# Thirty-six more small matmuls on a constant, around the first key tile of the first mixer

## Chip, core and metric

One core of a Trainium2 chip runs the whole program. The metric is the device time of one execution in microseconds, as the median of several runs. The engines are TensorE (PE; its weight loads are shown apart as PEld), VectorE (DVE), ScalarE (ACT), GpSimd (POOL) and SyncE (SP), which starts the transfers.

## What is computed

A decoder trunk of two layers for one sequence of 512 tokens and width 1024. The change lies in the first layer's mixer, sparse attention with an indexer: every query scores all earlier keys with eight small index heads, keeps the best 128 of them and attends to those.

```python
proj = rms_norm(x, norm_mix) @ w_in
q, k, v, qi, ki, wi, qm = _split(proj, A_SIZES)
logits = jnp.einsum('bqhd,bsd->bqhs', qib, ki)
score = jnp.einsum('bqhs,bqh->bqs', jax.nn.relu(logits), wib)
score = jnp.where(key_pos <= t_pos, score, NEG)
_, idx = lax.top_k(score, n_sel)
# attention of q over the chosen k, v; four more heads attend to 256 memory tokens
x = x + jnp.concatenate([mix, mo], axis=-1) @ w_out
x = x + swiglu_ffn(rms_norm(x, norm_ffn), w_gate_up, w_down)
```

All inputs and the output are float32.

## The kernel before

Activations lie transposed, 128 features by 512 tokens a tile, eight tiles (`KT`) for the width. A projection to 128 output features is eight accumulation steps over `KT` into one PSUM bank. There are two ways to do it. `fp32_steps` (L207) multiplies in float32 directly; the trace has two records for each such matmul. `proj_steps` (L235 to L237) splits weight and activation into a high and a low part, `wh`, `wl`, `xh`, `xl`, rounded for the fast float32 mode, and does three matmuls for each of the eight steps: `xh·wh`, `xl·wh`, `xh·wl`. The split of a weight is `_split2`: ScalarE casts the high part (L48), VectorE or GpSimd subtracts to get the low part (L51). `proj_steps` is a generator that stops after every second step, so after six matmuls, a quarter of the product.

`layer0` runs so: 14 small matmuls of `ones` by `ones` (L738) while the first loads are under way; five index projections in float32 (`product`, results `pk`, `pq`, `p1`, `p2`, `p3`); meanwhile the scaled input `x` is split into `xh` and `xl` (`halves`). Then comes the first tile of attention keys: `rope_steps(K, kb[:, 0], tag="O")` makes the product of 24 matmuls into the PSUM bank `psO` and turns it by the rotary angles (L374 to L384: five ScalarE copies out of PSUM, then GpSimd). The first four stops of `steps` are that product; it is the loop over `itertools.islice(steps, 4)`.

After it, the value product (`token_major`, L441 to L443, into `psT`) is woven with the index logits (`logits`, L452 into `psacc` and `psS`): for each of four pairs of heads and three query blocks two matmul groups, a ScalarE relu in PSUM (L789) and a VectorE update of the score (L791, L793). Between them stand the sums of squares of the memory tokens (L278, L256 to L265) and the row made of them (L288, L290). When the score is complete, VectorE runs 16 rounds of top-k (L727, L728) while PE does the next projections, the memory heads and the queries.

The order on PE is the order of the code. The other engines' order comes from a scheduler that lays the program out by a model of its times; added PE work can shift what it puts where. PSUM tags are pools: `acc` has two banks, `S` three, `T` two, `O` one. Split weights rotate through three `wh` and three `wl` buffers, raw weights through two `wf` buffers.

Of the kernel before, what the change touches and what calls it, by code (L numbers as in the profile page):

```python
# [53 lines left out]
def _weave(a, b, na=1, nb=1):  # L54

    live = True
    while live:
        live = False
        for g, n in ((a, na), (b, nb)):
            for _ in range(n):  # L60
                if next(g, g) is not g:
                    live = True


class _Trunk:
# [667 lines left out]

    def layer0(self):
        nc, mm = self.nc, self.nc.tensor.matmul
        idle = self.psum("T")
        for _ in range(14):
            mm(idle[:, :128], self.ones, self.ones, start=True, stop=True)  # L738
        x, parts = self.scaled(0)
        ws = itertools.chain(self.first, self.plain_chunks("in0", [2, 3, 4]))  # L740

# [35 lines left out]
        def logits(j):  # L777
            for i in (1, 2, 3):
                n = (i + 1) * 128
                sc = score[i]  # L780
                q = slice(j * 512 + i * 128, j * 512 + (i + 1) * 128)
                tag = ("S", "acc")[(j + i) % 2]
                ps = [self.psum(tag) for _ in range(2)]
                self.scores([(ps[s][:, :n], qi, None, ki, None, slice(s * 64, s * 64 + 64), q, slice(0, n))
                             for s in range(2)])
                for s in range(2):
                    t = ps[s]
                    w = wi[:, i, 2 * j + s:2 * j + s + 1]
                    nc.scalar.activation(t[:, :n], t[:, :n], AF.Relu)  # L789
                    if j + s == 0:  # L790
                        nc.vector.tensor_scalar(sc[:, :n], t[:, :n], w, None, op0=ALU.mult)  # L791
                    else:
                        nc.vector.scalar_tensor_tensor(sc[:, :n], t[:, :n], w, sc[:, :n], op0=ALU.mult, op1=ALU.add)  # L793
                if j == 3:
                    nc.gpsimd.affine_select(out=sc[:, i * 128:n], in_=sc[:, i * 128:n], pattern=[[-1, 128]],
                                            compare_op=ALU.is_ge, fill=NEG, base=0, channel_multiplier=1)
                yield 1
# [26 lines left out]
        steps = itertools.chain(rope_steps(K, kb[:, 0], tag="O"), value_steps())  # L824
        mem_parts = self.memory_squares(mem)
        every = itertools.chain.from_iterable(logits(j) for j in range(4))
        for _ in itertools.islice(steps, 4):
            pass
        _weave(itertools.islice(steps, 3), itertools.islice(every, 6), nb=2)
        self.mem_cols = self.ssq_cols(mem_parts, n=2, keep=True)  # L830
        _weave(itertools.islice(steps, 3), every, nb=2)
# [552 lines left out]
```

## Time and profile before

| | us |
|---|---|
| median of 3 runs | 1238.37 (1238.08 to 1239.43) |
| profiled execution | 1237.89 |
| its span, first to last instruction | 1236.0 |
| PE busy | 1196.5 (97%) |
| PEld busy | 944.8 (76%) |
| DVE busy | 529.3 (43%) |
| ACT busy | 484.1 (39%) |
| POOL busy | 350.2 (28%) |

The mean granted TensorE clock is 0.992 of full speed. PE's busy share is close to the span, so the places to read are the few in which PE waits, and the stretches in which its clock is granted at half. A matmul's recorded time is longer than the step to the next one, because matmuls overlap in the pipeline; the step from start to start is what it costs in a row of matmuls.

### The profile page before, as it was taken

The page shows a single profiled execution, that of the slowest core. Times are in us where ns is not written, and L with a number is a line of the kernel's source. Part 1 is how long each engine was busy: PE and PEld are TensorE (multiplying, and loading weights), DVE is VectorE, ACT ScalarE, POOL GpSimd, SP SyncE. Part 2 cuts the span into 40 slices and gives each one's busy share as a digit, 9 for nine tenths or more (in the row PEclk, how much of TensorE's full clock was granted, in tenths as well). Part 3 has the DMA queues.
Part 4 walks back from the last instruction along what each step waited for, and adds up shares of the span by engine and source line. Part 5 has one row for each costly group of instructions (what it writes and reads, how often), then busy time and mean ns, then how long its engine had stood idle before and what let it go on. Part 6 is the DMA issues. An engine that isn't in the chain of part 4 may idle for free.

```text
span 1236.0 us, 14342 instructions
## 1 busy us (share of the span) xinstructions
PE 1196.5 (97%) x5624; PEld 944.8 (76%) x5624; DVE 529.3 (43%) x1022; ACT 484.1 (39%) x852; POOL 350.2 (28%) x220
## 2 busy tenths in 40 slices
PE   9799899999999999999999999998999999999997
PEld 5367576578788888888888778886788888888886
DVE  4769724547433333332224543559433333331112
ACT  3663584424423323222222776545323223222222
POOL 0444453245222122212222323324322122211222
PEclk9899999999999999999999999999999999999999
DMA  5313103102322222222233121211222222222221
GB/s 189 130 38 132 57 35 95 59 34 92 110 76 99 102 102 103 79 96 94 94 115 113 58 69 34 83 55 69 91 82 100 103 103 101 77 87 94 94 94 69
DMA packets 29185, 108.36 MB, mean 88 GB/s; under 512 B 2494, under 2 KB 11582, under 8 KB 20670
## 3 DMA queue, kind: packets, MB, share of 16 engines
q1 hardware_dynamic: 28574, 106.93, 24.6%
q8 instruction: 44, 0.72, 0.2%
q10 hardware_dynamic: 544, 0.52, 0.1%
q14 instruction: 23, 0.19, 0.0%
HBM read 104.43 MB, written 3.01 MB: 87 GB/s over the span
## 4 chain that ended last, share of the span: by engine, by line
PE 77%; DVE 10%; DMA 4%; issue 4%; ACT 3%; POOL 2%; SPq 0%; DVEq 0%; POOLq 0%; ACTq 0%
PE psS L249 5%; PE psS L247 5%; PE psS L248 5%; PE psT L249 3%; PE psT L247 3%; PE psT L248 3%; PE psacc L249 3%; PE psacc L247 3%; PE psacc L248 3%; PE psacc L222 3%; PE psacc L224 3%; PE psacc L223 3%; PE psS L222 3%; PE psS L224 3%; PE psS L223 3%
## 5 line engine op out<-in xcount | busy, mean ns | idle before, releaser
L51 POOL TENSOR_TENSOR wl<-wf,wh 128x1024 fp32r<-128x1024 f32 x92 | 222.7, 2422 | 618.9 <-ACT wh L48 567.4
L48 ACT CAST wh<-wf 128x1024 fp32r<-128x1024 f32 (+1 forms) x163 | 167.4, 1030 | 505.4 <-issue 156.1
L51 DVE TENSOR_TENSOR wl<-wf,wh 128x1024 fp32r<-128x1024 f32 (+1 forms) x84 | 99.4, 1184 | 80.0 <-ACT wh L48 80.0
L249 PE MATMUL psS<-xh,wl 128*128 128x512 f32 x272 | 106.9, 393 | 0.0
L247 PE MATMUL psS<-xh,wh 128*128 128x512 f32 x272 | 106.5, 392 | 0.0
L248 PE MATMUL psS<-xl,wh 128*128 128x512 f32 x272 | 106.1, 390 | 0.0
L247 PE MATMUL psacc<-xh,wh 128*128 128x512 f32 x192 | 75.5, 393 | 0.6 <-DVE xT L653 0.6
L247 PE MATMUL psT<-xh,wh 128*128 128x512 f32 x192 | 75.5, 393 | 0.0
L249 PE MATMUL psT<-xh,wl 128*128 128x512 f32 x192 | 75.5, 393 | 0.0
L249 PE MATMUL psacc<-xh,wl 128*128 128x512 f32 x192 | 75.5, 393 | 0.0
L248 PE MATMUL psT<-xl,wh 128*128 128x512 f32 x192 | 74.9, 390 | 0.0
L248 PE MATMUL psacc<-xl,wh 128*128 128x512 f32 x192 | 74.9, 390 | 0.0
L316 POOL TENSOR_TENSOR ssq<-ssq,t 128x512 f32<-128x512 f32 (+1 forms) x31 | 41.0, 1322 | 96.6 <-ACT t L306 61.1
L248 PEld LDWEIGHTS psS<-xl,wh 128*128 128x128 f32 x272 | 51.1, 188 | 11.6
L249 PEld LDWEIGHTS psS<-xh,wl 128*128 128x128 f32 x272 | 51.1, 188 | 11.1
L247 PEld LDWEIGHTS psS<-xh,wh 128*128 128x128 f32 x272 | 51.1, 188 | 10.7
L235 PE MATMUL psacc<-xh,wh 128*128 128x512 f32 x136 | 58.1, 428 | 0.0
L668 DVE TENSOR_TENSOR raw<-psacc,R 128x512 f32<-128x512 f32 x22 | 15.2, 691 | 96.9 <-PE psacc L249 96.9
L237 PE MATMUL psacc<-xh,wl 128*128 128x512 f32 x136 | 54.1, 398 | 0.0
L236 PE MATMUL psacc<-xl,wh 128*128 128x512 f32 x136 | 54.0, 397 | 0.0
L653 DVE TENSOR_TENSOR xT<-xT,psacc 128x512 f32<-128x512 f32 x44 | 30.0, 683 | 39.0 <-PE psacc L224 38.9
L247 PEld LDWEIGHTS psacc<-xh,wh 128*128 128x128 f32 x192 | 36.1, 188 | 8.7 <-issue 1.2
(320 smaller groups left out, 2628.8 us busy)
## 6 DMA issues: line engine op xcount, KB each, us to landing
wf<-in_gu SPq DMA_DIRECT2D x44, 1024.0 KB
wf<-in_dn SPq DMA_DIRECT2D x16, 1024.0 KB
wf<-in_in SPq DMA_DIRECT2D x12, 1024.0 KB
wf<-in_dn SPq DMA_DIRECT2D x16, 384.0 KB
wf<-in_v SPq DMA_DIRECT2D x3, 1024.0 KB
wf<-in_in SPq DMA_DIRECT2D x5, 512.0 KB
xT<-in_x SPq DMA_DIRECT2D x8, 256.0 KB
wf<-in_mk SPq DMA_DIRECT2D x2, 1024.0 KB
```

The source lines that it names most:

```text
L48: nc.scalar.copy(hi, src)
L51: lo_engine.tensor_tensor(out=lo, in0=src, in1=hi.bitcast(F32), op=ALU.subtract)
L222: mm(out, wh[k], xh[k], start=first and k == 0, stop=False)
L223: mm(out, wh[k], xl[k], start=False, stop=False)
L224: mm(out, wl[k], xh[k], start=False, stop=last and k == n - 1)
L235: mm(out, wh[:, s], xh[k], start=k == 0, stop=False)
L236: mm(out, wh[:, s], xl[k], start=False, stop=False)
L237: mm(out, wl[:, s], xh[k], start=False, stop=k == KT - 1)
L247: mm(out, wh[:, s], xh[k], start=k == 0, stop=False)
L248: mm(out, wh[:, s], xl[k], start=False, stop=False)
L249: mm(out, wl[:, s], xh[k], start=False, stop=k == KT - 1)
L316: engine.tensor_tensor(out=parts[part], in0=parts[part], in1=sq, op=ALU.add)
```

## The change

The small matmuls of `ones` by `ones` become a helper, `keep_awake(tag, n)`, which takes a PSUM bank of the given tag and does `n` of them. It is called as before at the start (14 in `psT`), then with 16 in a bank of `acc` ahead of the first key tile's product, and with 5 after each quarter of that product.

```diff
     def layer0(self):
         nc, mm = self.nc, self.nc.tensor.matmul
-        idle = self.psum("T")
-        for _ in range(14):
-            mm(idle[:, :128], self.ones, self.ones, start=True, stop=True)
+        def keep_awake(tag, n):
+
+            idle = self.psum(tag)
+            for _ in range(n):
+                mm(idle[:, :128], self.ones, self.ones, start=True, stop=True)
+
+        keep_awake("T", 14)
...
         every = itertools.chain.from_iterable(logits(j) for j in range(4))
+        keep_awake("acc", 16)
         for _ in itertools.islice(steps, 4):
-            pass
+            keep_awake("acc", 5)
         _weave(itertools.islice(steps, 3), itertools.islice(every, 6), nb=2)
```

Lines behind the change are four or five further down in the changed kernel. On PE, at the end of the index projections (`psT<-xg,wf` is the last of them, `psO` the key product), the program now reads:

```order
L207 MATMUL psT<-xg,wf 128x512 x8
L740 MATMUL psacc<-ones 128x128 x16
L235 MATMUL psO<-xh,wh 128x512
L236 MATMUL psO<-xl,wh 128x512
L237 MATMUL psO<-xh,wl 128x512
L235 MATMUL psO<-xh,wh 128x512
L236 MATMUL psO<-xl,wh 128x512
L237 MATMUL psO<-xh,wl 128x512
L740 MATMUL psacc<-ones 128x128 x5
```

The six rows of the product and the five behind them come four times in all, and the fourth five stand ahead of the first `L441`. The first of the sixteen, and the first of the second, third and fourth five, waits for PE's own earlier work on its bank. Before, the `L740` rows are not there and the rest is the same.

On ScalarE, behind the casts of the value weights, before (names in brackets are the engines and transfers that an instruction waits for):

```order
L48 CAST wh<-wf 128x1024 [waits DMAHW6_49]
L48 CAST wh<-wf 128x1024
L374 COPY raw<-psO 128x512 [waits DMAHW4_49,PE_49,Pool_49]
L379 COPY raw<-psO 32x512 [waits DMAHW5_49,Pool_49]
L379 COPY raw<-psO 32x512 x3
L48 CAST wh<-wf 128x1024 [waits DMAHW7_49,DVE_49]
L789 ACTIVATE psacc<-psacc 128x256 [waits PE_49] x2
```

and in the change, where the copies and the relus have other line numbers in part:

```order
L48 CAST wh<-wf 128x1024 [waits DMAHW6_49]
L48 CAST wh<-wf 128x1024
L48 CAST wh<-wf 128x1024 [waits DMAHW7_49,DVE_49,PE_49]
L374 COPY raw<-psO 128x512 [waits DMAHW4_49,PE_49,Pool_49]
L379 COPY raw<-psO 32x512 [waits DMAHW5_49,Pool_49]
L379 COPY raw<-psO 32x512 x3
L793 ACTIVATE psacc<-psacc 128x256 [waits PE_49] x2
```

The cast for the second key tile has moved ahead of the five copies out of `psO`, and now waits for PE as well.

On VectorE, in the logits of the third pair of heads (`rs_q` and `rs_keep` belong to the memory tokens' norm), before:

```order
L263 TENSOR_TENSOR rs_q<-rs_keep 128x2
L793 SCALAR_TENSOR_TENSOR score<-psacc,wi,score 128x256
L264 SCALAR_TENSOR_TENSOR rs_q<-rs_v,rs_q 128x2
L793 SCALAR_TENSOR_TENSOR score<-psacc,wi,score 128x256
L265 SCALAR_TENSOR_TENSOR rs_keep<-rs_q,rs_keep 128x2
L793 SCALAR_TENSOR_TENSOR score<-psS,wi,score 128x384
L263 TENSOR_TENSOR rs_q<-rs_keep 128x2
L793 SCALAR_TENSOR_TENSOR score<-psS,wi,score 128x384
L264 SCALAR_TENSOR_TENSOR rs_q<-rs_v,rs_q 128x2
L265 SCALAR_TENSOR_TENSOR rs_keep<-rs_q,rs_keep 128x2
L288 TENSOR_SCALAR raw<-ident,rs_keep 128x128 x2
```

and in the change:

```order
L263 TENSOR_TENSOR rs_q<-rs_keep 128x2
L264 SCALAR_TENSOR_TENSOR rs_q<-rs_v,rs_q 128x2
L265 SCALAR_TENSOR_TENSOR rs_keep<-rs_q,rs_keep 128x2
L263 TENSOR_TENSOR rs_q<-rs_keep 128x2
L264 SCALAR_TENSOR_TENSOR rs_q<-rs_v,rs_q 128x2
L265 SCALAR_TENSOR_TENSOR rs_keep<-rs_q,rs_keep 128x2
L288 TENSOR_SCALAR raw<-ident,rs_keep 128x128 x2
L797 SCALAR_TENSOR_TENSOR score<-psacc,wi,score 128x256 x2
L797 SCALAR_TENSOR_TENSOR score<-psS,wi,score 128x384 x2
```

The four score updates have moved behind the whole column chain. GpSimd does the low part of the second key tile's weight ahead of the turn of the first key tile; ScalarE also does one copy of values earlier among scalings of the memory tokens. All other rows of all engines, and SyncE's transfers, keep their order.

## Rows read from the trace of the kernel before

**Rows 1.** The page, part 1: busy us, share of the span, instructions.

```profile
PE 1196.5 (97%) x5624; PEld 944.8 (76%) x5624; DVE 529.3 (43%) x1022; ACT 484.1 (39%) x852; POOL 350.2 (28%) x220
```

**Rows 2.** Waits of PE: us in total, times, longest.

```profile
PE psT L469 <- ACT frow L485: 4.3, 3, 2.8
PE psO L235 <- ACT wh L48: 4.2, 1, 4.2
PE psO L237 <- DVE wl L51: 2.8, 1, 2.8
```

**Rows 3.** Timeline of PE: start us, us, operation, [idle before <- what ended it].

```profile
36.97 0.41 PE L770 MATMUL psS<-ident,o 8*128 8x8 f32 x4
38.91 8.83 PE L207 MATMUL psT<-xg,wf 128*128 128x512 f32 x16 [1.53 <-DMA wf<-in_in]
51.91 0.50 PE L235 MATMUL psO<-xh,wh 128*128 128x512 f32 x1 [4.17 <-ACT wh L48]
...
55.45 0.80 PE L237 MATMUL psO<-xh,wl 128*128 128x512 f32 x1 [2.80 <-DVE wl L51]
...
59.73 0.39 PE L235 MATMUL psO<-xh,wh 128*128 128x512 f32 x1
...
62.48 0.28 PE L441 MATMUL psT<-wh,xh 128*128 128x256 f32 x1
```

**Rows 4.** Windows: busy us (count) by engine, PEclk, DMA share, GB/s.

```profile
38.90:42.40 3.50, 3.49 (x5) 1.43 (x6) 2.39 (x3) 3.39 (x7) 0.72 (x1) 0.53 0.30 114
...
55.45:59.45 4.00, 4.00 (x9) 3.13 (x10) 4.00 (x6) 0.00 (x0) 3.02 (x3) 0.50 0.74 264
59.53:62.48 2.95, 2.95 (x14) 2.42 (x13) 1.23 (x2) 2.00 (x2) 0.21 (x1) 1.00 0.85 347
...
146.40:149.10 2.70, 0.00 (x0) 0.00 (x0) 0.00 (x0) 2.64 (x6) 2.70 (x2) 1.00 0.00 0
149.10:152.00 2.90, 2.85 (x14) 1.78 (x16) 1.38 (x2) 1.12 (x2) 2.88 (x4) 1.00 0.98 315
```

**Rows 5.** Small and fp32 matmuls: PE timeline (two rows), windows of `ones` on PE.

```profile
1.12 5.20 PE L738 MATMUL psT<-ones 128*128 128x128 f32 x28 [1.12 <-DVE eps L1212]
30.01 7.03 PE L207 MATMUL psT<-xg,wf 128*128 128x512 f32 x16
...
1.10:4.90 3.80, 3.78 (x17) 1.00 0.67 206
4.90:6.20 1.30, 1.30 (x13) 1.00 0.89 282
```

**Rows 6.** Timeline of PE where fast and fp32 matmuls alternate.

```profile
122.03 0.40 PE L237 MATMUL psacc<-xh,wl 128*128 128x512 f32 x1
122.36 0.70 PE L452 MATMUL psS<-km,qm 64*128 64x256 f32 x2
```

**Rows 7.** Timeline of ScalarE behind the key product.

```profile
62.73 0.59 ACT L374 COPY raw<-psO 128x512 f32<-128x512 f32 x1 [0.54 <-issue]
63.34 2.34 ACT L379 COPY raw<-psO 32x512 f32<-32x512 f32 x4
65.71 1.05 ACT L48 CAST wh<-wf 128x1024 fp32r<-128x1024 f32 x1
66.78 0.65 ACT L789 ACTIVATE psacc<-psacc 128x256 f32<-128x256 f32 x2
```

**Rows 8.** Timeline of PE in the logits.

```profile
67.73 1.30 PE L452 MATMUL psacc<-ki,qi 64*128 64x512 f32 x3 [0.82 <-DVE score L791]
...
73.06 0.91 PE L452 MATMUL psacc<-ki,qi 64*128 64x384 f32 x2 [1.56 <-DVE score L791]
```

**Rows 9.** Timeline of VectorE in the logits and at the start of top-k.

```profile
79.09 0.48 DVE L793 SCALAR_TENSOR_TENSOR score<-psacc,wi,score 128x256 f32<-128x256 f32 x1 [0.24 <-ACT psacc L789]
...
82.59 1.62 DVE L793 SCALAR_TENSOR_TENSOR score<-psacc,wi,score 128x512 f32<-128x512 f32 x2 [0.30 <-ACT psacc L789]
...
88.61 1.48 DVE L727 MAX8 m<-score 128x8 f32<-128x512 f32 x3 [0.40 <-POOL score L795]
```

## Prediction
> **What bounds the kernel now.** I read the page first, then TensorE's (PE's) list of waits, then its timeline from 38 to 75 us with the granted clock of the same stretches. PE is busy for 1196.5 of 1236.0 us [rows 1], so a microsecond put on PE's queue is a microsecond on the end, unless it falls into one of the few waits. Two of the longest lie right where the change puts its matmuls [rows 2]: 4.2 us ahead of the first matmul of the key tile's product (ScalarE's `wh`) and 2.8 us ahead of its third (VectorE's `wl`). The timeline shows them in place [rows 3]: the last index product ends at 38.91 + 8.83 = 47.74 us, the key product starts at 51.91, and its third matmul, which reads `wl`, starts at 55.45. The remaining 22 of its 24 matmuls then take 55.45 to 62.48 = 7.03 us. They do not run at one speed: up to 59.5 us the granted clock is 0.50 (1.2 GHz), after that 1.00 (2.4 GHz) [rows 4]. At full clock a step is 0.23 us (59.73 to 62.48 is 12 matmuls), so 22 would take 5.06 us. The low clock costs 7.03 - 5.06 = **1.97 us** here. That is all that keeping PE awake can bring in this place.
>
> **The change part by part.** It adds 36 fp32 matmuls of 128 columns to PE's queue, 16 ahead of the product and 5 behind each quarter of it (six matmuls), and removes nothing. Nothing reads them, so they cost PE time alone.
>
> *Price of one.* The kernel's own 14 at the start leave 28 records, two each [rows 5]. 17 records fit in the first 3.80 us and 13, edges included, in the next 1.30 us: 0.22 us a record while PE is slow, 0.10 when it is fast. An fp32 product of 512 columns, whose 16 records take 7.03 us at full clock (0.44 each) [rows 5], gives 0.11 for a quarter of the columns. I take 0.11, so 0.22 us for one small matmul at full clock and 0.44 at half.
>
> *The 16 ahead.* 32 x 0.11 = 3.5 us, inside the 4.17 us in which PE waits for `wh` anyway: cost 0. If PE were at half clock they would take 7.0 us and reach past 51.91, but the third matmul still waits for `wl` until 55.45; the two ahead of it would end near 55.6. So 0 to 0.2 us.
>
> *The 20 between and behind.* From 55.45 on PE waits for nothing before 62.48. No wait covers these, so all of it lies on the path: 40 x 0.11 = **4.4 us** (4.0 by the 0.10).
>
> *Going over between the two kinds.* A step from an L237 matmul to an fp32 one is 0.33 us instead of 0.23 [rows 6]; I take as much for the way back. Four groups, eight changes, 0.1 each at most: 0 to 0.8 us. I take 0.5.
>
> *The clock.* Here I have to choose. The rows have a wait of 2.7 us, from 146.4 to 149.1, after which the clock is still 1.00, and one of only 1.53 us, ahead of 38.91, after which it is 0.53 over 3.5 us [rows 3, 4]. Before the first PE ran a mix of fast matmuls and transposes; before the second it ran an fp32 product and then four transposes of 8 columns [rows 3, 5]. The new position resembles the second: fp32 matmuls, a gap under 1 us, two key matmuls, and then the unchanged 2.8 us wait for `wl`, in front of which the change puts nothing, since its next five come only after the sixth matmul. So I expect one more fall, in that wait or just behind it, and a stretch at half clock as short as the one from 38.9 (0.53 over 3.5 us is 3.3 us at half). Half of what lies behind 55.45 is lost: 0.85 us where the fall comes early in the wait, 1.65 where it comes after. I take 1.4 in place of the 1.97 lost now, a gain of 0.6 us.
>
> The Trainium skill, TensorE: Matmul & The Clock Gate, in its table "Why this matters for your kernels", blames idle gaps between bursts of matmuls for such drops. Taken alone, that rule makes a filled gap a kept clock, and the sum would be that of the second case below; the 1.53 us row against the 2.7 us row speaks against idle time as the only cause.
>
> *What the scheduler moved.* On VectorE four updates of the score now stand behind five column operations and two `L288`: some 1.4 us later, against 0.24 and 0.30 us of VectorE idle [rows 9]. They hold PSUM buffers that the next logits want: 0 to 0.9 us, I take 0.2, since VectorE catches up at its next wait. On ScalarE the cast of the next key tile's `wh` now stands ahead of the five copies out of `psO`. It waits for PE, because the third `wh` buffer is the one the key product reads until its end. Copies and cast, 1.05 us [rows 7], then follow the product as they do now, in the other order; cost 0.
>
> *What waits behind.* ScalarE's relus start at 66.78, behind copies and cast without a break [rows 7], and PE's waits of 0.82 and 1.56 us among the logits go back to them through VectorE [rows 8]. All of it starts from the product's end, so it moves with it. VectorE's top-k starts at 88.61, just behind the last logits [rows 9], and later waits of PE, the 2.8 us at 149 among them [rows 2], hang on it. I find no cover for the delay.
>
> **Sum:** 4.4 + 0.5 + 0.2 - 0.6 = **+4.5 us**. The profiled execution took 1237.89 us (span 1236.0): 1242.4. The median of the runs shown is 0.48 us higher, so I predict **1242.9 us**. With the low ends (4.0, 0, 0, and 0.85 lost of 1.97) it is +2.9, with the high ends (4.4, 0.8, 0.9, 0.2 for the sixteen and 1.65 lost) +6.0; most of this case lies between 1241.5 and 1244.3.
>
> **The rivals.** *The clock holds through the wait.* For it: 146.4 to 149.1. Then all 1.97 us come back: 4.4 + 0.5 - 1.97 = +2.9, with VectorE's 0.2 +3.1, 1241.5 us. Still slower, because twenty small matmuls cost 4.9 us and the clock can return no more than 1.97; it would take a price of 0.1 us a piece to break even.
>
> *The delay falls into waits that stand there already, and the kernel is not slower.* The place is the logits: PE waits 0.82 and 1.56 us there [rows 8]. If ScalarE's relus did not move with the product (the cast, 1.05 us, done under it, and the copies not the last thing they wait for), PE would lose up to 2.4 us of waiting instead of adding it: +0.7 with the clock held, +2.1 without, 1239 to 1240.5 us. It decides at the first relu: at 66.8 us this case holds, at 71 the first. Against it: the cast's wait for PE, and the copies that read `psO`.
>
> *Dearer than counted.* The first of three of the groups waits for PE itself, and PE is at half clock as long as now. A matmul's time of 0.39 us against a step of 0.23 [rows 3, 6] makes 0.16 us for each emptied pipeline. 4.4 + 0.8 + 0.5 + 0.9 and the full 1.97 lost again gives +6.6 us, 1245.0.
>
> *Faster*: it would need small matmuls that cost PE nothing behind 55.45. The records of the first fourteen, one behind the other, say no.
>
> **How the numbers follow.** The fall with +4.5: 0.50. The clock held, +3.1: 0.25. Taken up by the waits: 0.14. Dearer: 0.08. Faster: 0.03. A measurement of this kernel can tell 0.2%, 2.5 us, from no change, so slower means above 1240.85 us. That holds for nearly all of the first two cases, the dearer one and a small part of the third: 0.82. Same is 0.15, faster 0.03. The range 1239.8 to 1244.7 takes in the first two, the upper half of the third and leaves out most of the dearer case and the gain.
>
> The Trainium skill, the same page, section "What's actually happening", says that the number of matmuls run at the low clock differs from run to run of one kernel; a single profile here cannot show that.
>
> **What would show it.** Right: 16 small matmuls from 47.7 to about 51.2 us; the third key matmul still at 55.45 behind `wl`; four groups of about 1.1 us (more at half clock) in the product; `L441` first at about 66.8 us instead of 62.48; the relus and the first MAX8 later by the same 4 to 5 us; a stretch at 0.50 that ends near 60 us. The clock step is wrong if PEclk stays 1.00 from 51.9 to the product's end (then `L441` at about 65.4). The path is wrong if the product ends late and MAX8 still starts near 88.6.

## The result, and the profile after

| | before | the change |
|---|---|---|
| median of 6 runs, us | 1239.62 (1238.08 to 1242.37) | 1246.95 (1246.33 to 1247.95) |
| ratio to before | | 1.0054, interval [1.0035, 1.0074] |
| profiled execution, us | 1237.89 | 1247.08 |

The change makes the kernel slower, by more than the forecast of 1242.9 us and outside its range. One execution is not like the next here: 110 executions of the kernel before, taken beside the experiments below, lie between 1236.46 and 1246.29 us with a median of 1241.45, so the three times that the prediction started from lie in the lower part of that spread, and so does the profiled execution. Beside executions of its own chip and hour the change stands at 1246.66 us against 1241.52 (12 and 29 executions, ratio 1.0045 [1.0028, 1.0062]; `after_again` below). By the means it is 1246.64 against 1240.84 with all 41 executions of the kernel before of that hour: **+5.8 us**.

The page of the changed kernel, part 1, in the columns of [rows 1]:

```profile
PE 1209.2 (97%) x5696; PEld 957.0 (77%) x5696; DVE 529.8 (43%) x1022; ACT 484.3 (39%) x852; POOL 349.9 (28%) x220
```

72 records more on PE, two for each of the 36 matmuls, and 12.7 us more of PE time; the other engines are as before. Where PE waits, in the columns of [rows 2]:

```profile
PE psO L237 <- DVE wl L51: 2.8, 1, 2.8
...
PE psO L235 <- ACT wh L48: 2.3, 1, 2.3
...
PE psacc L452 <- DVE score L795: 1.7, 1, 1.7
```

The wait for `wh` has shrunk from 4.2 to 2.3 us, since the sixteen stand in it; the wait for `wl` is the 2.8 us it was. PE's timeline over the stretch of [rows 3]:

```profile
37.52 7.13 PE L207 MATMUL psT<-xg,wf 128*128 128x512 f32 x16 [0.60 <-DMA wf<-in_in]
44.49 3.73 PE L740 MATMUL psacc<-ones 128*128 128x128 f32 x32
50.53 0.50 PE L235 MATMUL psO<-xh,wh 128*128 128x512 f32 x1 [2.30 <-ACT wh L48]
...
54.06 0.80 PE L237 MATMUL psO<-xh,wl 128*128 128x512 f32 x1 [2.80 <-DVE wl L51]
...
55.94 2.33 PE L740 MATMUL psacc<-ones 128*128 128x128 f32 x10
57.92 0.66 PE L235 MATMUL psO<-xh,wh 128*128 128x512 f32 x1
...
59.58 1.27 PE L740 MATMUL psacc<-ones 128*128 128x128 f32 x10
60.61 0.48 PE L235 MATMUL psO<-xh,wh 128*128 128x512 f32 x1
...
64.57 1.28 PE L740 MATMUL psacc<-ones 128*128 128x128 f32 x10
65.61 0.37 PE L441 MATMUL psT<-wh,xh 128*128 128x256 f32 x1
...
75.01 2.14 PE L452 MATMUL psacc<-ki,qi 64*128 64x384 f32 x3 [1.74 <-DVE score L795]
```

From the third key matmul to the first `L441` it is now 65.61 - 54.06 = 11.55 us, where it was 7.03 [rows 3]: **+4.52 us**. A group of five takes 1.03 us from start to start at full clock (59.58 to 60.61) and 1.98 at half (55.94 to 57.92). The wait that [rows 8] has at 67.73 (0.82 us) is gone; the second one is there, 1.74 us at 75.01. The first reason to look for is on ScalarE, where the cast and the copies have changed places (the lines that answer to [rows 7]):

```profile
64.54 1.04 ACT L48 CAST wh<-wf 128x1024 fp32r<-128x1024 f32 x1 [3.66 <-PE psO L236]
65.61 0.59 ACT L374 COPY raw<-psO 128x512 f32<-128x512 f32 x1
66.22 2.34 ACT L379 COPY raw<-psO 32x512 f32<-32x512 f32 x4
68.59 0.65 ACT L793 ACTIVATE psacc<-psacc 128x256 f32<-128x256 f32 x2
```

The cast waits for the product's last `L236`, not for the five small matmuls behind it, so it runs beneath them (64.54 to 65.58 against 64.57 to 65.61). The first relu starts 68.59 - 65.61 = 2.98 us after the first `L441`, where it was 66.78 - 62.48 = 4.30 [rows 3, 7]: 1.3 us of the delay are taken back. Most of it is not the exchange itself: in `ahead16` (below), which has the new order on ScalarE but no small matmuls in the product, the relu starts 4.03 us after the first `L441`. So the exchange is worth some 0.3 us, and the other 1.0 are the last five, which hold up PE while ScalarE needs only the product.

TensorE's clock in windows of the changed kernel, in the columns of [rows 4]:

```profile
51.50:58.30 6.80, 4.24 (x15) 3.85 (x16) 6.66 (x9) 1.91 (x4) 5.58 (x5) 0.50 0.46 162
75.40:85.60 10.20, 10.20 (x33) 5.88 (x31) 6.68 (x23) 3.19 (x7) 0.00 (x0) 0.50 0.00 0
225.60:229.00 3.40, 3.40 (x10) 0.77 (x8) 1.64 (x6) 1.85 (x5) 1.82 (x2) 0.50 0.02 7
816.10:819.50 3.40, 3.40 (x10) 2.71 (x10) 0.69 (x1) 0.00 (x0) 2.34 (x2) 0.50 0.00 0
```

The first one is the stretch at half clock that the prediction expected in the wait for `wl`. The second lies in the logits and was not expected. In the profiled execution of the kernel before, the same stretch ran at full clock, and that kernel has a fall at 677.4 us that this one has not:

```profile
75.00:85.20 10.20, 10.20 (x67) 7.36 (x65) 8.51 (x26) 5.88 (x14) 0.00 (x0) 1.00 0.01 2
677.40:680.80 3.40, 3.40 (x9) 2.65 (x9) 2.20 (x9) 0.90 (x2) 1.29 (x1) 0.50 0.93 282
```

Compared trace with trace, the changed kernel is 3.1 us early at the last index product (no fall at 39 us, a DMA wait of 0.60 in place of 1.53), 3.1 us late after the key product, 6.4 us late behind the stretch of 75 to 86 us, and 9.2 us late at the end. The first MAX8 shows it, at 94.96 us instead of 88.61 [rows 9]:

```profile
94.96 1.48 DVE L727 MAX8 m<-score 128x8 f32<-128x512 f32 x3 [0.40 <-POOL score L799]
```

Read from these two traces alone, the stretch at 75 us looks like the change's doing. The experiments had to say whether it is.

### The profile page after: what moved, and what is told of

It is laid out like the page before. It is cut to its first block, busy times and chain, and to the rows that moved or that the text cites. A ratio compares the mean times of both kernels' runs of the same rounds, so it can differ in the third digit from the quotient of the medians.

```text
span 1245.2 us, 14485 instructions
## 1 busy us (share of the span) xinstructions
PE 1209.2 (97%) x5696; PEld 957.0 (77%) x5696; DVE 529.8 (43%) x1022; ACT 484.3 (39%) x852; POOL 349.9 (28%) x220
## 3 DMA queue, kind: packets, MB, share of 16 engines
q1 hardware_dynamic: 28574, 106.93, 24.7%
## 4 chain that ended last, share of the span: by engine, by line
PE 78%; DVE 10%; issue 3%; DMA 3%; ACT 3%; POOL 2%; SPq 0%; DVEq 0%; POOLq 0%; ACTq 0%
PE psS L249 5%; PE psS L247 5%; PE psS L248 5%; PE psT L249 3%; PE psT L247 3%; PE psT L248 3%; PE psacc L249 3%; PE psacc L247 3%; PE psacc L248 3%; PE psacc L222 3%; PE psacc L224 3%; PE psacc L223 3%; PE psS L222 3%; PE psS L224 3%; PE psS L223 3%
## 5 line engine op out<-in xcount | busy, mean ns | idle before, releaser
L236 PE MATMUL psacc<-xl,wh 128*128 128x512 f32 x136 | 53.3, 392 | 0.0
```

The lines of the kernel that those rows point to most:

```text
L236: mm(out, wh[:, s], xl[k], start=False, stop=False)
```

## The experiments

Two theories stand against each other. **Theory 1:** the twenty small matmuls behind the third key matmul cost what they take, and the rest is the spread of one kernel's times. **Theory 2 (rival):** the change brings new falls of the clock, in the logits above all, or the scheduler's moved rows cost time. The first batch below was forecast from theory 2, that the change makes the fall in the logits; theory 1 was set up after its times, with `before_again`. For each kernel I also give the mean granted clock over all its executions as time at half clock, 2 x (1 - granted clock) x span, and the span less half of that, which is what the span would be at full clock. Both are rough: the clock is listed to 0.001, which is 1.2 us of such a span, and half-clock time in which PE only waits costs nothing and is taken off all the same. The kernels ran in four batches, each on one chip beside executions of the kernel before: `ahead16`, `between20`, `in_wait` and `after_fill` (35 executions of the kernel before); `before_again`, `after_again`, `double` and `fill_only` (29, or 41 with `before_again`); `early_vw` and `in_wait_early_vw` (23); the last two (23). Each new kernel has 12 executions, `double` 6. Unless a diff says otherwise, `keep_awake` is the change's helper, with its 14 at the start.

**One part of the change alone.**

`ahead16`, from the change:

```diff
         for _ in itertools.islice(steps, 4):
-            keep_awake("acc", 5)
+            pass
```

> Only the 16 small matmuls ahead of the key tile, none in its product. Theory (the added matmuls in the product cost 4.5 us there, and the longer half-clock stretch in the logits, 75.4 to 85.6 us in the trace of the change, costs about 3 us more, which comes from PE's waits there): the 16 lie in PE's wait for wh and cost nothing; the product from its third matmul takes 7 us as before; the whole is 1238 to 1241 us, no more than 0.1% from the kernel before. Rival (the scheduler's new order costs the time): the cast of the next key tile and VectorE's chain of column operations move here too, so it is slower than before by 3 us or more, near 1243.

`between20`, from the change:

```diff
-        keep_awake("acc", 16)
         for _ in itertools.islice(steps, 4):
             keep_awake("acc", 5)
```

> Only the four groups of 5 in and behind the product, no 16 ahead. Theory: third key matmul to first value matmul takes 11.5 us instead of 7.0, and the logits fall to half clock as in the change: 5.5 to 7.5 us slower than before, near 1246. Rival (order): VectorE's order is that of the kernel before here, ScalarE's cast is moved; if VectorE's chain makes the loss in the logits, it stays at +4.5, near 1244.

Measured: `ahead16` 1242.69 us, ratio 1.001 [0.9993, 1.0028]; `between20` 1245.64, ratio 1.0036 [1.0015, 1.0057]; the kernel before 1241.6 (1236.46 to 1246.1). The twenty carry the loss. The sixteen gain nothing and may cost a little: the interval allows -0.9 to +3.5 us. By the means the two parts add up, 1.6 + 4.2 = 5.8 us, as much as the whole change. Neither theory was met in full: `ahead16` lies above the 1238 to 1241 us that were expected, and `between20`, 4.0 us above the kernel before by the medians, lies under the 5.5 to 7.5 us of its theory and near the 4.5 us of its rival, that VectorE's moved rows make the loss in the logits. That rival is taken up below. `ahead16` has the sixteen that fill part of the first wait, and its trace still has the 2.81 us wait for `wl` and a stretch at half clock from 53.8 to 60.6 us. The end of its product and its first relu, for the 4.03 us above (66.65 - 62.62):

```profile
62.62 0.28 PE L441 MATMUL psT<-wh,xh 128*128 128x256 f32 x1
...
66.65 0.65 ACT L793 ACTIVATE psacc<-psacc 128x256 f32<-128x256 f32 x2
```

**The same kernels again, and twice the dose.**

`before_again` is the kernel before, `after_again` the change, both unedited. `double`, from the change:

```diff
-            keep_awake("acc", 5)
+            keep_awake("acc", 10)
```

> The kernel before once more, for a second profile of it and for the spread of one and the same kernel. Theory (a stretch at half clock among the logits comes in some executions of every version, the trace of before shown first had none, and that trace and its few runs were on the low side): the runs spread over 5 us or more, the mean is near 1241, and the profile may well show a stretch at 0.50 between 70 and 90 us. Rival (the half-clock stretch in the logits belongs to the change): no stretch at 0.50 between 70 and 90 us, runs within 2 us of each other.

> The change once more, against the same runs of before on one chip. Theory (20 uncovered small matmuls cost 4.5 us, the clock gives nothing back on average, the rest of the first difference was the draw of the executions): mean 4 to 5.5 us above before, near 1246. Rival (the change also makes the clock fall in the logits, every time): 7 us above before, near 1248, and all runs at a mean clock of 0.988 or less.

> The change with 10 small matmuls behind each quarter instead of 5. Theory (each uncovered small matmul is paid in full): 20 more at 0.21 us, 4.2 to 4.6 us slower than the change, near 1250. Rival (waits behind take delay up, or the cost is a fixed one for breaking the stream): 0 to 2 us slower than the change.

| | median us | ratio to before | half-clock us, mean | span at full clock, mean |
|---|---|---|---|---|
| before_again | 1240.8 (1236.97 to 1246.68) | 0.999 [0.9973, 1.0007] | 26.2 | 1225.9 |
| after_again | 1246.66 (1243.43 to 1248.97) | 1.0045 [1.0028, 1.0062] | 29.2 | 1229.9 |
| double | 1251.21 (1245.26 to 1252.94) | 1.0068 [1.0042, 1.0094] | 28.3 | 1234.3 |

With the other executions of the kernel before in the batch, its span at full clock is 1225.5 us. So 1225.5, 1229.9, 1234.3: each twenty small matmuls add 4.4 us (5.1 and 4.6 by the medians). This measure alone does not price the twenty, since by it `in_wait` (below), whose small matmuls all stand in waits, is 3.7 us above the kernel before of its batch. The traces do price them. In `double`, PE's timeline and the clock of the product's first part are:

```profile
55.63 0.80 PE L237 MATMUL psO<-xh,wl 128*128 128x512 f32 x1 [2.83 <-DVE wl L51]
...
72.43 0.37 PE L441 MATMUL psT<-wh,xh 128*128 128x256 f32 x1
...
55.63:61.50 5.87, 5.87 (x23) 5.50 (x24) 4.12 (x7) 1.11 (x2) 3.01 (x3) 0.50 0.82 307
```

From the third key matmul to the first `L441`, less half of the time at half clock, `double` takes 16.80 - 5.87/2 = 13.9 us, the change 11.55 - 4.24/2 = 9.4 and the kernel before 5.0 (7.03 less half of some 4.1). Each twenty cost **4.4 to 4.5 us** at full clock there, with all going over between the two kinds. The profile of the kernel before, taken a second time, shows what the stretch in the logits is (windows of `before_again`):

```profile
51.20:61.40 10.20, 6.32 (x14) 4.58 (x15) 9.21 (x13) 4.64 (x8) 6.75 (x6) 0.50 0.40 149
75.00:85.20 10.20, 10.12 (x33) 6.05 (x32) 5.46 (x16) 3.29 (x8) 0.00 (x0) 0.50 0.01 2
225.20:228.60 3.40, 3.40 (x12) 0.77 (x8) 1.59 (x6) 1.93 (x5) 1.83 (x2) 0.51 0.01 2
815.70:819.10 3.40, 3.40 (x10) 2.74 (x9) 0.69 (x1) 0.00 (x0) 2.23 (x2) 0.51 0.02 5
```

The unchanged kernel falls at 75, 225 and 816 us too, just where the changed one did, and this execution of it took 1246.68 us, as long as the changed one's 1247.08. The falls there need no change; whether the change makes them more frequent is not shown. Which set of falls an execution gets differs from one to the next, and one kernel's times spread over 10 us. This trace also answers the rival of the moved rows on VectorE:

```profile
68.14 0.64 ACT L789 ACTIVATE psacc<-psacc 128x256 f32<-128x256 f32 x2
...
94.50 1.48 DVE L727 MAX8 m<-score 128x8 f32<-128x512 f32 x3 [0.40 <-POOL score L795]
```

From the first relu to the first MAX8 the kernel before takes 94.50 - 68.14 = 26.36 us here and the changed kernel, with the moved rows, 94.96 - 68.59 = 26.37, both with 10.2 us at half clock. The moved rows cost nothing in these two.

Half-clock time is 27 us on the mean for the kernel before and 29.5 for the change (18 executions): 2.5 us more, half of which is 1.2 us of time. The spread leaves its size open.

The second profile of the change, of `after_again`, differs from the first in the product:

```profile
55.66 0.51 PE L237 MATMUL psO<-xh,wl 128*128 128x512 f32 x1 [2.84 <-DVE wl L51]
...
66.84 0.36 PE L441 MATMUL psT<-wh,xh 128*128 128x256 f32 x1
...
52.45:55.65 3.20, 0.37 (x2) 0.00 (x0) 3.20 (x6) 2.50 (x5) 3.10 (x3) 1.00 0.00 0
57.20:60.60 3.40, 3.40 (x14) 2.92 (x13) 2.55 (x5) 0.05 (x1) 1.46 (x2) 0.50 0.91 376
```

Here the clock was 1.00 through the open wait and fell only behind it, among the small matmuls and the product's second quarter, for 3.4 us. The stretch from the third key matmul to the first `L441` is 11.18 us instead of 11.55.

**Small matmuls where PE waits.**

`after_fill`, from the change, with three and six small matmuls ahead of the two logits that waited in the profile; `fill_only`, the same nine in the kernel before:

```diff
+        fill = {(0, 3): 3, (1, 2): 6}
         def logits(j):
...
+                if (j, i) in fill:
+                    keep_awake("O", fill[j, i])
                 ps = [self.psum(tag) for _ in range(2)]
```

> The change, with small matmuls also in the logits: 3 ahead of the first pair of heads' third block and 6 ahead of the second pair's second block, into the bank psO, where PE waits for VectorE's scores. Theory: PE's clock stays 1.00 through the logits (no stretch at 0.50 from 75 to 86 us), the 9 cost at most 1 us of uncovered time: 2 to 3.5 us faster than the change, near 1244. Rival (order, or the path is ScalarE's and VectorE's and not PE's clock): the same time as the change, 1247, or 1 to 2 us more.

> The kernel before with nothing but the 9 small matmuls in the logits (3 and 6, into psO), where PE waits 0.8 and 1.6 us; the other engines keep the order of before. Theory (the half-clock stretch among the logits is what such matmuls can take away, since they lie in waits): no stretch at 0.50 between 70 and 90 us in the profile, 1 to 3 us faster than before in the mean, near 1239. Rival (the loss in the logits comes from the scheduler's order): no difference from before; or, if the 9 aren't covered, 1 us slower.

Measured: `after_fill` 1242.42 us, 1.0017 [1.0003, 1.0032], with 23.8 us at half clock; `fill_only` 1242.03, 1.0004 [0.9989, 1.0019], with 29.6. On top of the change the nine seem to take back some 3.6 us (by the means +2.2 us over the kernel before of their batch, against +5.8 in the other batch), with 5.7 us less at half clock; on top of the kernel before they give nothing, where 1 to 3 us were expected. In both traces the stretch at 75 us is gone, but `fill_only` falls at 126, 150, 222 and 812 us instead. A fall that is kept away in one place need not lower the sum.

`in_wait`, from the kernel before: the sixteen ahead, and twelve between the second and the third key matmul, in the wait for `wl` that the change leaves open:

```diff
-    def proj_steps(self, out, w, xh, xl):
+    def proj_steps(self, out, w, xh, xl, gap=None):
...
+            if k == 0 and gap is not None:
+                gap()
...
-        steps = itertools.chain(rope_steps(K, kb[:, 0], tag="O"), value_steps())
+        steps = itertools.chain(rope_steps(K, kb[:, 0], tag="O", gap=lambda: keep_awake("acc", 12)), value_steps())
...
+        keep_awake("acc", 16)
```

> 16 ahead, none behind the quarters, but 12 between the second and the third matmul of the product, where PE waits 2.8 us for wl. Theory: 12 x 0.21 = 2.5 us lie in the wait, the clock stays at 1.00 through the product, which takes 5.1 us from its third matmul instead of 7.0: 2 us faster than before, near 1237.6, if the logits keep their clock. Rival (the clock falls whatever PE does with small matmuls, because they don't count): a stretch at 0.50 in the product as before, time as before, 1239.6. Rival (order): slower by 1 us or more.

Measured: 1242.17 us, ratio 1.0008 [0.9991, 1.0026]: no gain, where 2 us were expected. Its PE timeline, with the clock of the product:

```profile
52.06 2.84 PE L742 MATMUL psacc<-ones 128*128 128x128 f32 x24
...
60.92 0.39 PE L443 MATMUL psT<-wh,xh 128*128 128x256 f32 x1 [0.55 <-ACT wh L48]
...
62.18 0.38 PE L445 MATMUL psT<-wl,xh 128*128 128x256 f32 x1 [0.76 <-DVE wl L51]
...
55.04:60.20 5.16, 5.16 (x22) 4.05 (x22) 4.14 (x6) 0.38 (x1) 3.05 (x3) 1.00 0.81 277
```

and ScalarE's in the same stretch: the two casts of the values' weights, the cast for the second key tile, and the first relu:

```profile
59.82 1.99 ACT L48 CAST wh<-wf 128x1024 fp32r<-128x1024 f32 x2 [5.40 <-DMA wf<-in_vw]
...
62.58 1.05 ACT L48 CAST wh<-wf 128x1024 fp32r<-128x1024 f32 x1 [0.77 <-DMA wf<-in_in]
...
66.64 0.64 ACT L795 ACTIVATE psacc<-psacc 128x256 f32<-128x256 f32 x2
```

The product ran at full clock (1.00 in the trace from 55.04 to 60.20 us) and ended some 2 us earlier than at half clock, and then PE waited 0.55 and 0.76 us for the values' weights, which came by DMA only at 59.8 us. Of the two microseconds that a full clock can return in this place, 1.3 fall into this new wait. ScalarE too had to wait for a weight: the cast for the second key tile, now ahead of the copies, started only at 62.58, and the first relu came 66.64 - 55.04 = 11.60 us after the third key matmul, no sooner than in the kernel before (66.78 - 55.45 = 11.33 [rows 3, 7]).

**The values' weights loaded early.**

`early_vw`, from the kernel before, and `in_wait_early_vw`, from `in_wait`:

```diff
-    def token_weights(self, src, n, deep=False):
+    def token_weights(self, src, n, deep=False, w=None):
...
-        w = self.load(src, [KT * n])
+        w = self.load(src, [KT * n]) if w is None else w
...
+        vw = self.big("vw", F32)
+        nc.sync.dma_start(vw, self.io["vw0"])
...
-            w = self.token_weights(self.io["vw0"], 256)
+            w = self.token_weights(None, 256, w=vw)
```

> The kernel before, with the values' weights loaded at the start into a buffer of their own instead of into a rotating one just ahead of the key tile; no small matmul is added. Theory (the values' weights swallow what a full clock would give): alone it changes little, since in the kernel before the product ends at 62.5 us and the casts of these weights are done by then: within 2 us of the kernel before, with no wait of PE at the value product's first matmuls. Rival (the values' weights bind nothing, only the clock's chance falls differ): no difference, and none in the next kernel either. Third way: the casts come earlier and hold the split-weight buffers that the key tile wants, its wait for wh grows past 4.2 us and the kernel is 1 to 3 us slower.

> Sixteen small matmuls ahead of the key tile and twelve between its second and third matmul, none in the rest of the product, and the values' weights loaded at the start. Theory: the key product runs at full clock (third matmul at about 55, first value matmul at about 60.3 us), the waits of 0.55 and 0.76 us at the value product's first matmuls are gone, and the time is 1.5 to 2 us under the kernel with the early load alone, so 1239 to 1240 where the kernel before has 1241. Rival (only the sum of half-clock stretches counts, and it falls elsewhere instead): the product at full clock, but the time within 0.7 us of the other kernel, with half-clock time per execution no less on the mean.

`in_wait_early_again` is the second of them once more, and `in_wait_early_fill` adds to it:

```diff
+        fill = {(0, 3): 10, (1, 2): 6}
```

> The same kernel once more: sixteen small matmuls ahead of the key tile, twelve in the wait for wl, none in the rest of the product, values' weights loaded at the start. Theory (the full clock in the product is kept and nothing swallows it any longer): 1239 us again, 1 to 2.5 us under the kernel before in the same call. Rival (the first time was a draw from the spread): 1240.5 to 1242, no difference from before.

> The same, and ten small matmuls in the wait of 2.7 us and six in that of 1.6 us among the logits, so that PE waits nowhere long between the key tile and the top-k. Theory: these lie in waits and cost nothing, the stretch at half clock that began at 67.3 us goes, which took up the second of these waits: 0 to 1 us under the kernel without them. Rival (the falls are not made by these waits but come again at another place): no difference, the stretch at half clock shows up elsewhere, or the six take their 1.3 us.

| | median us | before, same batch | ratio | half-clock us, mean |
|---|---|---|---|---|
| early_vw | 1241.96 (1237.22 to 1246.2) | 1240.37 | 1.0013 [0.9997, 1.003] | 29.1 |
| in_wait_early_vw | 1239.07 (1236.08 to 1242.47) | 1240.37 | 0.9989 [0.9973, 1.0006] | 16.5 |
| in_wait_early_again | 1238.7 (1237.07 to 1243.29) | 1242.4 | 0.9975 [0.9958, 0.9992] | 16.7 |
| in_wait_early_fill | 1239.55 (1236.06 to 1241.31) | 1242.4 | 0.9982 [0.9966, 0.9999] | 19.4 |

(Half-clock time of the kernel before in the two batches: 24.7 and 28.4 us.) The early load alone gives nothing. With the two waits filled it gives 2.9 us against `early_vw` in the same batch (2.6 by the means), a little more than was expected. No other kernel here is measurably faster than this one: it is 1.3 and 3.7 us under the kernel before by the medians of the two batches, 1.9 by the means of both together, with the second interval wholly below 1 and the first reaching to 1.0006. The sixteen more in the logits change nothing that can be told. PE's timeline of `in_wait_early_vw`:

```profile
45.46 3.73 PE L742 MATMUL psacc<-ones 128*128 128x128 f32 x32
51.51 0.51 PE L235 MATMUL psO<-xh,wh 128*128 128x512 f32 x1 [2.32 <-ACT wh L48]
...
52.09 2.84 PE L742 MATMUL psacc<-ones 128*128 128x128 f32 x24
55.08 0.51 PE L239 MATMUL psO<-xh,wl 128*128 128x512 f32 x1 [0.15 <-DVE wl L51]
...
60.24 0.28 PE L443 MATMUL psT<-wh,xh 128*128 128x256 f32 x1
```

The twelve fill the wait for `wl` to 0.15 us, the product takes 60.24 - 55.08 = 5.16 us instead of 7.03 [rows 3], and the value product starts without a wait. The early load may also have brought the second key tile's weight sooner; no run separates the two. That the clock is kept there in every execution is not so. The profiled execution of `in_wait_early_again` fell in the filled wait itself (two rows of PE, then windows, the first one on the 2.30 us for `wh` that stay open):

```profile
51.73 4.47 PE L742 MATMUL psacc<-ones 128*128 128x128 f32 x24
55.96 0.48 PE L239 MATMUL psO<-xh,wl 128*128 128x512 f32 x1
...
48.90:51.10 2.20, 0.00 (x0) 0.00 (x0) 2.20 (x3) 2.16 (x4) 1.31 (x1) 1.00 0.08 32
51.90:55.30 3.40, 3.40 (x18) 3.40 (x18) 3.40 (x5) 3.33 (x6) 3.40 (x4) 0.50 0.00 0
```

That is not free. From the first of the twelve to the third key matmul it is 55.96 - 51.73 = 4.23 us instead of 2.99 (52.09 to 55.08), so 1.2 of the 1.97 us are lost again; the 22 matmuls behind have the full clock.

All fourteen profiles can be set side by side. In the ten that leave the wait for `wl` open, 3.4 to 5.9 us of the stretch from the third key matmul to the first value matmul ran at half clock; in the four in which the twelve fill it, none did. The mean time at half clock, 16.6 us over 24 executions, is 8 to 12 us under that of the kernel before.

## Why the prediction was wrong

**Right:** the sign, the place and the price of the twenty. The sum had 4.4 + 0.5 - 0.6 = 4.3 us from the third key matmul to the first `L441`; the trace has 4.52. A group measured 1.03 us where 1.1 was counted, and the traces give 4.4 to 4.5 us for twenty at full clock. That 4.3 and 4.52 lie so close is in part luck: the 0.5 us for going over between the two kinds was nearly all too much, and the 0.6 us from the clock did not come. The third matmul still started on `wl` behind a 2.80 us wait, the sixteen took 3.73 us inside the wait for `wh`, and a stretch at 0.50 ended at 58.3 us, where "near 60" was said.

**The steps that failed, in order of size:**

*The base.* "The profiled execution took 1237.89 us ... the median of the runs shown is 0.48 us higher", and "a measurement of this kernel can tell 0.2%". Of 110 executions of this kernel, 27 in 100 lie under 1238.4 us; their mean is 1241.0. The sum was set on a base 2.6 us too low; the same +4.5 us on 1241.0 gives 1245.5. I had three times within 1.4 us and took that for the spread; the real one is ten microseconds wide, and the trace alone could not show it. The Trainium skill, TensorE: Matmul & The Clock Gate, section "What's actually happening", says of a kernel's start that the number of matmuls at the low clock differs from run to run. That sentence stood behind the sum as a remark and did not widen the range; the two profiles of the kernel before, 1237.89 and 1246.68 us with different falls, show that it should have.

*The clock*, "a gain of 0.6 us". In the profiled execution 4.24 us of the product ran at half clock (54.06 to 58.30), which costs 2.1 us and not the 1.4 I took, against 1.97 before: no gain. In the second profiles of both it is 1.7 us (3.4 at half clock) for the change and 2.6 for the kernel before (5.1, 56.3 to 61.4 us), so the product alone may gain a little. Over all executions of the change, half-clock time was 2.5 us above the mean of the kernel before, about +1.2 us where -0.6 was counted, at the edge of what the spread lets one say. The forecast priced the clock in the product alone; where else the 1.2 us lie, no run shows. The reason given, that the change puts nothing in front of the wait for `wl`, fits all fourteen profiles (some half clock in the product in the ten with that wait open, none in the four that fill it); the size I put on it was off. `in_wait_early_vw`, which does fill that wait, has 1.87 of the 1.97 us back (7.03 to 5.16).

*"I find no cover for the delay"*. The last five of the twenty stand behind the product, and ScalarE waits for the product alone: cast and copies did not move by those five, and the relus came 1.3 us sooner after the first `L441` than before. This is the second rival's mechanism, and a part of its 2.4 us: its first relu was to start at 66.8 us, the first case's at 71, and it started at 68.59 in an execution that was 1.4 us early at the third key matmul, so 70.0 on the forecast's clock (69.83 in `after_again`, whose third key matmul is 0.2 us late). The 0.2 us for VectorE's moved rows measured nothing (26.36 against 26.37 us). The forecast's own sum did not have this gain. The mean span at full clock, +4.4 us, does not show the gain either: 4.5 less 1.3 would be 3.2.

*The end.* +4.4 us at full clock and +1.2 for the clock make 5.6, and 5.8 was measured beside the kernel before. Both parts are cut from the same measured spans, so that they add up is no proof of either. The 9.2 us between the two profiled executions are in good part two draws: against `before_again`, an execution of the kernel before with the same falls behind the product and 6.8 us more at half clock up to it (one more fall at 41 us, and 10.2 us about the product instead of 6.8), the changed kernel's was only 0.4 us longer. One pair of profiles says as little as the other.

**The other rivals.** *The clock holds through the wait* did not happen in the change's first profile (0.50 from 51.5 to 58.3 us). In the second, `after_again`, the clock did hold through the wait, 1.00 to 55.65 us, but then fell for 3.4 us in the product, so the 1.97 us did not come back there either. *Dearer than counted*, +6.6 us, came near the total for another reason: the groups were not dearer, and the total stood on a higher base. *Faster* is excluded by the interval.

**Still open:** why the sixteen alone, in a wait, stand at +1.1 us by the medians. Their interval reaches from below zero, and their trace shows no later third matmul (54.80 us). Open too is the 1.2 us between the 3.2 that the traces account for and the 4.4 of the means at full clock; as said above, that span is a rough measure.

## What to carry to other kernels

In this kernel filler matmuls paid only where PE had to wait, and only when they filled the wait directly ahead of the work to be sped up; put behind it, among matmuls that wait for nothing, they cost their full time. What is won by a faster clock has to meet data that is ready; here none of it showed until the values' weights were loaded sooner. And where the clock decides a few microseconds, take many executions of the base before naming what a change is worth, and compare means of half-clock time, not two profiles.

## What the runs showed of the hardware

- One unchanged program on one core took 1236.46 to 1246.68 us in 122 executions on four chips (1237.22 to 1246.29 in 23 on one of them), with a mean granted clock between 0.985 and 0.992. Two profiled executions of it had different sets of half-clock stretches (39, 53 and 677 us; 41, 51, 75, 225 and 816 us).
- Idle time is not the only thing that goes before a fall. In the first profile of the kernel before, PE was recorded busy for 7.11 of the 7.40 us ahead of 677.4 us, at full clock, with fast matmuls and then four of two columns, and the clock fell to 0.50:

```profile
670.00:677.40 7.40, 7.11 (x30) 5.65 (x29) 6.00 (x18) 1.63 (x2) 1.61 (x1) 1.00 0.77 237
...
675.54 1.80 PE L278 MATMUL psacc<-ones,ssq 128*128 128x2 f32 x8
```

The Trainium skill, TensorE: Matmul & The Clock Gate, table "Why this matters for your kernels", names idle gaps between bursts of matmuls for such drops; this fall does not fit that. In `in_wait_early_again` the clock was still 1.00 while PE idled for 2.2 us, and 0.50 in the busy 3.4 us that followed.
- A small fp32 matmul of 128 columns costs 0.21 us in a row at full clock (1.03 for five) and 0.40 at half (1.98 for five). Twenty in groups of five among fast matmuls cost 4.4 to 4.5 us at full clock, 0.22 each with the going over.
